# Gate products of the RG-LRU's tiles 0 to 5 on the two halves of the array's rows, their results brought to place by DMA

## The chip, the core and the metric

The kernel runs on one core of a Trainium2 chip. The metric is the device time of one execution in microseconds. A NeuronCore has a matrix engine (TensorE; PE in the profile, PEld for its weight loads), VectorE (DVE), ScalarE (ACT), GpSimd (POOL) and SyncE (SP), which issues the DMAs of this kernel. Each engine takes its instructions in the order of its own list. On-chip data lie in SBUF over 128 partitions; products land in PSUM, also 128 partitions.

## The reference, cut to what matters

One decoder layer over 1024 tokens and 1024 channels: a norm, an input projection, an S5 branch and an RG-LRU branch side by side, a gated merge, a SwiGLU feed-forward and a final gate. The change touches the RG-LRU branch alone. It works on 16 heads of 64 channels:

```python
xh = xc.reshape(bsz, L, LRU_HEADS, LRU_HEAD_DIM)          # 16 heads of 64
r = sigmoid(einsum('blhi,hij->blhj', xh, w_r) + b_r)
ig = sigmoid(einsum('blhi,hij->blhj', xh, w_i) + b_i)
log_a = -LRU_C * r * softplus(-lru_lambda)
a = exp(log_a)
bx = sqrt(-expm1(2.0 * log_a)) * ig * xh
h = scan(h -> a * h + bx)                                  # over the tokens
```

## The kernel before, in words

Channels lie on partitions, tokens on the free axis, so a tile is 128 channels by 1024 tokens, and the RG-LRU's 1024 channels are 8 tiles m of two heads each. A matrix product in full precision is made of three fp32r products (`mm3`, line 220): high part by high part, high by low and low by high, each in two pieces of 512 tokens. Weights come as 128x512 pieces: SP loads one (line 169), ACT makes its high part (195), DVE its low part (196).

A unit is one output tile: its products on PE, and behind them its evacuation `ev`, which is written into the program one unit later. For the gates of tile m, `ri_mm` (599) makes 12 products of 128x512 into two PSUM tiles of 1024 columns: one for r, one for i. Each weight block is 128x128 with the two heads' 64x64 matrices on its diagonal and zeros elsewhere. `ev_ri` (608) applies the two sigmoids (612) out of PSUM. After every odd m, `lru` (618) runs for the tiles m-1 and m: exponentials on ACT (623), tanh (626), squares (629), products on DVE (632, 634), square roots on ACT (636), a product (639) and the scan (643) on DVE, then a store of the scanned tile to DRAM for m below 6, which is read back later (722).

The order of the units around the change: input tile `ub` m (its 48 products, then u at 536 and 587, the convolution xc at 589 and 592 on DVE, and the split xch, xcl at 239 and 240), gates of tile m-2 (`RI_LAG` = 2), and after m = 2, 3, 5 and 6 one merge-gate tile. At the end come the gates of tile 6, a merge gate, the gates of tile 7, and the rest. The w_b_out products (from line 779) need all eight scanned tiles.

PSUM has four tiles of 1024 columns, shared by all units; a unit of the gates takes two. SBUF has 43 slots for tiles of 1024 columns, and five buffers each for the high and low weight parts. A framework puts the instructions of each engine, and the DMAs of SP, into one fixed list when the program is built, from times that it expects; at run time each engine takes its list in order and waits on semaphores. SP's list holds the weight loads too, and a load waits until the buffer that it fills has been read.

Of the kernel before, what the change touches and what calls it, by code (L numbers as in the profile page):

```python
# [14 lines left out]
AF = mybir.ActivationFunctionType  # L15
ALU = mybir.AluOpType

P = 128
L = 1024
# [14 lines left out]
GATES_FIRST = 10  # L34
UB_GATES = (2, 3, 5, 6)
RI_LAG = 2
S5_LAG = 4
S5_STAGGER = 3
X_POOL = ()
# [11 lines left out]
_n = 0  # L51
for _name, _cols in (
    ("g_mix", 8), ("b_in", 28), ("b_glu", 4), ("conv_w", 32), ("conv_b", 8),
    ("b_r", 8), ("b_i", 8), ("lam", 8), ("g_ffn", 8), ("g_pg", 8), ("b_pg", 8),
    ("g_ple", 8), ("g_fin", 8),
):
    VEC[_name] = _n
    _n += _cols
# [44 lines left out]
class Build:  # L103
# [343 lines left out]
    def plan(self):  # L447
        nc, h = self.nc, self.h
# [133 lines left out]
        xcs, xct, ri, yb = {}, {}, {}, {}  # L582
# [14 lines left out]
            return ev  # L597

        def ri_mm(m):
            def mm(u, hi, lo, pairs):  # L600
                u.ps = [self.ps_sm(), self.ps_sm()]
                for q in range(2):
                    w = slice((2 * (m % 2) + q) * P, (2 * (m % 2) + q + 1) * P)
                    self.mm3(u.ps[q], hi[:, w], lo[:, w], xcs[m], True, True)
                xcs.pop(m)
            return mm

        def ev_ri(m):
            def ev(ps):
                for q, b in ((0, "b_r"), (1, "b_i")):  # L610
                    t = self.slot(name="ri")
                    nc.scalar.activation(out=t, in_=ps[q], func=AF.Sigmoid, bias=self.v(b, m))  # L612
                    ri[m, q] = t
                if m % 2 == 1:
                    self.lru_last = self.start(lru(m - 1))
            return ev
# [33 lines left out]
        ri_elem = {}  # L650

        def add_ub(m):
# [3 lines left out]
                    self.lrup = self.start(self.lru_params())  # L656
            self.add(w_in(4 + m), ev_ub(m), pre=pre)

        def add_ri(m):
            if m // 2 not in ri_elem:  # L660
                ri_elem[m // 2] = self.elem(h["w_ri"][m // 2])
            self.add([(ri_elem[m // 2], None)], ev_ri(m), mm=ri_mm(m))


        ya, gl, mg, ybs = {}, {}, {}, {}
# [80 lines left out]
        for m in range(8):  # L746
            if m:
                add_ub(m)
            if m >= RI_LAG:
                add_ri(m - RI_LAG)  # L750
            if m in UB_GATES:
# [684 lines left out]
    def s5_data(self, hf):  # L1436
# [80 lines left out]
        yield  # L1517


INS = ("xT", "pT", "vec", "ident", "iota", "s5p", "s5bc", "s5d", "w_ple", "w_in", "w_ri", "w_glu", "w_a_out",  # L1520
       "w_b_out", "w_o", "w_gate", "w_up", "w_down", "w_pg")


# [6 lines left out]
def layout(a):  # L1530

    f = {}
    f["xT"] = np.ascontiguousarray(a["x"][0].T).reshape(8, P, L)
    f["pT"] = np.ascontiguousarray(a["p"][0, 0].T).reshape(2, P, L)
    cols = {
        "g_mix": a["g_mix"], "b_in": a["b_in"], "b_glu": a["b_glu"], "conv_w": a["conv_w"], "conv_b": a["conv_b"],
        "b_r": a["b_r"], "b_i": a["b_i"], "lam": a["lru_lambda"], "g_ffn": a["g_ffn"], "g_pg": a["g_ple_gate"],
        "b_pg": a["b_ple_gate"], "g_ple": a["g_ple"], "g_fin": a["g_final"],
    }
    f["vec"] = np.ascontiguousarray(np.concatenate([cols[n].reshape(-1, P) for n in VEC], 0).T)  # L1540
    f["ident"] = np.eye(P, dtype=np.float32)
    f["iota"] = np.tile(np.arange(P, dtype=np.float32), (P, 1))
    pair = lambda v: v.reshape(16, 2, 64).transpose(1, 2, 0).reshape(P, 16)
    ldt = np.repeat(a["log_dt"][0][:, None], 64, axis=1)
    f["s5p"] = np.ascontiguousarray(np.concatenate([pair(a["lam_re"][0]), pair(a["lam_im"][0]), pair(ldt)], 1))
    pb = lambda v: v.reshape(16, 2, 64, 16).transpose(1, 2, 0, 3).reshape(P, 16, 16)
    f["s5bc"] = np.ascontiguousarray(np.stack(
        [pb(a["s5_b_re"][0]), pb(a["s5_b_im"][0]),
         pb(a["s5_c_re"][0].transpose(0, 2, 1)), pb(a["s5_c_im"][0].transpose(0, 2, 1))], 1))
    d = np.zeros((2, 16, 16, 16), np.float32)  # L1550
    for i in range(16):
        d[:, i, :, i] = a["s5_d"][0].reshape(16, 2, 16)[:, :, i].T
    f["s5d"] = d.reshape(32, 16, 16)
    f["w_in"] = strips(a["w_in"][0])
    wp = strips(a["w_ple"][0])
    f["w_ple"] = np.ascontiguousarray(wp.reshape(4, 2, P, 256).transpose(0, 2, 1, 3)).reshape(4, P, 512)
    ri = np.zeros((8, 2, 2, 64, 2, 64), np.float32)
    for q, n in enumerate(("w_r", "w_i")):
        w = a[n][0].reshape(8, 2, 64, 64)
        for i in range(2):  # L1560
            ri[:, q, i, :, i, :] = w[:, i]

    f["w_ri"] = np.ascontiguousarray(ri.reshape(4, 2, 2, P, P).transpose(0, 3, 1, 2, 4)).reshape(4, P, 512)
    for n, s in (("w_glu", "w_glu"), ("w_a_out", "w_a_out"), ("w_b_out", "w_b_out"), ("w_o", "w_o"),
                 ("w_gate", "w_ffn_gate"), ("w_up", "w_ffn_up"), ("w_down", "w_ffn_down"), ("w_pg", "w_ple_gate")):
        f[n] = strips(a[s][0])
    return f
# [16 lines left out]
```

## Time and profile before

| what | value |
|---|---|
| runs shown | 1465.94 us median of 3 (1462.96 to 1466.12) |
| the profiled execution's own time | 1471.47 us |
| its span, first to last instruction | 1469.7 us |
| mean granted TensorE clock | 0.978 |
| PE busy | 97% of the span |
| DVE busy, ACT busy | 58%, 38% |

Starts in the profile are microseconds from the first instruction. The units of the gates lie between 343 and 491 us. A row of a timeline gives the start, the busy time, the engine, the line, what is written from what, and in brackets the idle time before it with what ended it. The tile names: sm is a PSUM tile of the gates' products, mm that of other units, ri a gate tile, xch and xcl the parts of xc, whi and wlo those of a weight piece.

### The profile page before, as it was taken

To read this page: it belongs to the slowest core of one execution; us is meant where nothing else is said; L and a number is where in the kernel's file an instruction comes from. 1 tells how busy PE (TensorE), PEld (TensorE's weight loads), DVE (VectorE), ACT (ScalarE), POOL (GpSimd) and SP (SyncE) were. 2 spreads that over 40 slices of the span, in tenths; PEclk is the share of its full clock that TensorE was granted. 3 is DMA by queue.
4 is the path that set the end of the run, shared out by engine and by line. 5 is a ranking of instruction groups with operands and counts; after the bars stand their busy time and mean duration, and the time that the engine had idled before them with its cause. 6 is when DMAs were issued, how large, how long until landed. Compare 5 with 4: busy or idle time off the path is not lost.

```text
span 1469.7 us, 16824 instructions
## 1 busy us (share of the span) xinstructions
PE 1420.5 (97%) x6586; PEld 1175.7 (80%) x6586; DVE 848.3 (58%) x988; ACT 565.8 (38%) x722; POOL 165.6 (11%) x250
## 2 busy tenths in 40 slices
PE   8999989999988899998999999999999999999995
PEld 6788877888877688887888888888888888888884
DVE  7367872635666864366556555556666243266586
ACT  7233235413665832244433333333335341133342
POOL 7910700000000000000000000000000021012333
PEclk9999979999999999999999999999999999999997
DMA  8224324451212554352122222222217342233222
GB/s 336 93 101 117 106 67 139 139 211 59 86 58 87 192 180 150 122 172 101 43 84 75 86 86 86 87 86 86 86 65 278 128 157 65 74 104 111 65 79 115
DMA packets 72047, 167.70 MB, mean 114 GB/s; under 512 B 11712, under 2 KB 23392, under 8 KB 71968
## 3 DMA queue, kind: packets, MB, share of 16 engines
q1 hardware_dynamic: 71968, 166.62, 33.6%
q8 instruction: 52, 0.85, 0.2%
q14 instruction: 27, 0.22, 0.0%
HBM read 121.37 MB, written 44.04 MB: 113 GB/s over the span
## 4 chain that ended last, share of the span: by engine, by line
PE 79%; issue 5%; ACT 5%; DVE 5%; POOL 4%; SPq 1%; DMA 1%; DVEq 0%; POOLq 0%; ACTq 0%
PE mm L228 46%; PE mm L321 29%; PE sm L1505 1%; PE sm L1500 1%; PE sm L228 1%; POOL x L1004 1%; SPq L1404 1%; ACT ri L612 1%; POOL el L1066 0%; DVE yb L643 0%; DVE x L1067 0%; DVE xc L592 0%; SPq L1444 0%; DVE el L1057 0%; ACT a L623 0%
## 5 line engine op out<-in xcount | busy, mean ns | idle before, releaser
L195 ACT ACTIVATE whi<-raw 128x512 fp32r<-128x512 f32 (+1 forms) x158 | 97.2, 617 | 360.7 <-PE mm L228 302.4
L321 PE MATMUL mm<-twh,whi 128*128 128x512 f32 x528 | 206.7, 392 | 3.8 <-ACT twh L239 3.8
L321 PE MATMUL mm<-twl,whi 128*128 128x512 f32 x528 | 206.4, 391 | 0.0
L321 PE MATMUL mm<-twh,wlo 128*128 128x512 f32 x528 | 202.9, 391 | 0.0
L196 DVE TENSOR_TENSOR wlo<-raw,whi 128x512 fp32r<-128x512 f32 (+1 forms) x158 | 111.6, 708 | 136.2 <-ACT whi L195 135.6
L228 PE MATMUL mm<-xgh,whi 128*128 128x512 f32 x448 | 141.7, 398 | 4.4 <-ACT ri L612 4.4
L228 PE MATMUL mm<-xgh,wlo 128*128 128x512 f32 x448 | 139.3, 393 | 0.9 <-DVE wlo L196 0.9
L228 PE MATMUL mm<-xgl,whi 128*128 128x512 f32 x448 | 140.0, 393 | 0.0
L321 PEld LDWEIGHTS mm<-twh,whi 128*128 128x128 f32 x528 | 99.7, 189 | 25.2 <-ACT twh L239 4.3
L321 PEld LDWEIGHTS mm<-twl,whi 128*128 128x128 f32 x528 | 99.9, 189 | 20.9
L321 PEld LDWEIGHTS mm<-twh,wlo 128*128 128x128 f32 x528 | 99.7, 189 | 20.8
L424 POOL TENSOR_TENSOR acc<-acc,sq 128x1024 f32<-128x1024 f32 (+1 forms) x18 | 43.3, 2406 | 610.4 <-DMA raw<-w_down 465.3
L228 PE MATMUL mm<-vh,wlo 128*128 128x512 f32 x352 | 108.9, 390 | 0.0
L182 ACT ACTIVATE whi<-wr 128x512 fp32r<-128x512 f32 x110 | 69.4, 631 | 102.6 <-PE mm L321 98.8
L228 PE MATMUL mm<-vl,whi 128*128 128x512 f32 x352 | 108.4, 389 | 0.0
L228 PE MATMUL mm<-vh,whi 128*128 128x512 f32 x352 | 108.3, 389 | 0.0
L228 PEld LDWEIGHTS mm<-xgh,whi 128*128 128x128 f32 x448 | 85.1, 191 | 23.4 <-ACT ri L612 4.9
L228 PEld LDWEIGHTS mm<-xgl,whi 128*128 128x128 f32 x448 | 85.6, 191 | 18.3 <-issue 0.2
L228 PEld LDWEIGHTS mm<-xgh,wlo 128*128 128x128 f32 x448 | 84.8, 190 | 19.2 <-DVE wlo L196 1.3
L183 DVE TENSOR_TENSOR wlo<-wr,whi 128x512 fp32r<-128x512 f32 x110 | 74.5, 685 | 25.0 <-ACT whi L182 24.9
L228 PEld LDWEIGHTS mm<-vh,wlo 128*128 128x128 f32 x352 | 66.1, 188 | 14.0 <-issue 0.2
L228 PEld LDWEIGHTS mm<-vh,whi 128*128 128x128 f32 x352 | 66.1, 188 | 13.9 <-issue 0.2
(389 smaller groups left out, 2456.8 us busy)
## 6 DMA issues: line engine op xcount, KB each, us to landing
raw<-w_in SPq DMA_DIRECT2D x56, 256.0 KB, 2.7
wr<-w_gate SPq DMA_DIRECT2D x22, 512.0 KB, 5.1
wr<-w_up SPq DMA_DIRECT2D x22, 512.0 KB, 3.6
vd<-fv SPq DMA_DIRECT2D x22, 512.0 KB, 2.9
vr<-vd SPq DMA_DIRECT2D x22, 512.0 KB, 5.5
raw<-w_down SPq DMA_DIRECT2D x32, 256.0 KB, 2.7
el<-ed SPq DMA_DIRECT2D x16, 512.0 KB, 4.2
x<-xT SPq DMA_DIRECT2D x8, 512.0 KB, 7.1
```

Of the source, the lines that this page charges most:

```text
L182: nc.scalar.activation(out=hi, in_=src, func=AF.Copy)
L183: nc.vector.tensor_tensor(out=lo, in0=src, in1=hi.bitcast(F32), op=ALU.subtract)
L195: nc.scalar.activation(out=hi[:, :w], in_=raw[:, :w], func=AF.Copy)
L196: nc.vector.tensor_tensor(out=lo[:, :w], in0=raw[:, :w], in1=hi[:, :w].bitcast(F32), op=ALU.subtract)
L228: nc.tensor.matmul(ps[:, t - t0:e - t0], w, v[:, t:e], start=(first and q == 0), stop=(last and q == 2),)
L321: nc.tensor.matmul(bank[b], w[:, k * P:(k + 1) * P], v, start=start and k == 0 and p == 0, stop=k == 3 and p == 2, skip_group_check=True)
L424: eng.tensor_tensor(out=a, in0=a, in1=s, op=ALU.add)
L612: nc.scalar.activation(out=t, in_=ps[q], func=AF.Sigmoid, bias=self.v(b, m))
L1004: (nc.gpsimd if eng else nc.vector).tensor_tensor(out=x, in0=x, in1=rstd["z"][:, :TAIL_CUT], op=ALU.mult)
L1404: nc.sync.dma_start(km[i][16 * j:16 * j + 16, :, (7 - j) * 16:P], ks[16 * i:16 * i + 16, :, 0:(j + 1) * 16])
L1500: nc.tensor.matmul(ps[:, o:o + P], km[hh][:, pr, :], us[q][:, 2 * i + hh, :], start=True, stop=False)
L1505: nc.tensor.matmul(ps[:, o + 1:o + P], G(w[hs, pr]), x[hs, pr * P:pr * P + 127], start=False, stop=last)
```

## The change

For the tiles m = 0 to 5 (`RI_HALVES` = 6) the products no longer use the block-diagonal weights. The weight block of tile m, from a new input `w_rh`, holds head 0's matrices on rows 0 to 63 with r and i side by side in the columns, and head 1's on rows 64 to 127 with i first. Each product then takes 64 rows: rows 0 to 63 write one PSUM tile, rows 64 to 127 the other, in turns, so there are again 12 products of 512 columns, each with half the rows. A PSUM tile now holds one head's r and i on its two halves of partitions, with the bias from a new table `b_ri`. The sigmoids write into two new tiles rx, and four DMAs of 64 partitions by 4 KB (256 KB each) build the r tile and the i tile from them. Six tiles make 24 such DMAs. The tiles 6 and 7 stay as they were.

The new weights come in two pieces (tiles 0 to 3, and 4 and 5) in place of three; all of the gates' weight pieces now lie in slots (`keep`) from their load to their last use, and no longer in the weight buffers. The table of vectors grows by 16 columns.

```diff
+RI_HALVES = 6
...
+            def halves(u, hi, lo, pairs):
+
+                u.ps = [self.ps_sm(), self.ps_sm()]
+                c = slice((m % 4) * P, (m % 4 + 1) * P)
+                xh, xl = xcs.pop(m)
+                for p, (w, v) in enumerate(((hi, xh), (hi, xl), (lo, xh))):
+                    for t in range(0, L, 512):
+                        for i in range(2):
+                            k = slice(64 * i, 64 * i + 64)
+                            self.nc.tensor.matmul(u.ps[i][:, t:t + 512], w[k, c], v[k, t:t + 512],
+                                                  start=p == 0, stop=p == 2)
+            return halves if m < RI_HALVES else whole
...
+                if m < RI_HALVES:
+                    t = [self.slot(name="rx") for _ in range(2)]
+                    for i in range(2):
+                        nc.scalar.activation(out=t[i], in_=ps[i], func=AF.Sigmoid, bias=self.v("b_ri", 2 * m + i))
+                    for q in range(2):
+                        o = ri[m, q] = self.slot(name="ri")
+                        for i in range(2):
+                            j = 64 * (i ^ q)
+                            nc.sync.dma_start(o[64 * i:64 * i + 64], t[i][j:j + 64])
...
         def add_ri(m):
-            if m // 2 not in ri_elem:
-                ri_elem[m // 2] = self.elem(h["w_ri"][m // 2])
-            self.add([(ri_elem[m // 2], None)], ev_ri(m), mm=ri_mm(m))
+            e, w = (m // 4, h["w_rh"][m // 4]) if m < RI_HALVES else (2 + m // 2, h["w_ri"][m // 2])
+            if e not in ri_elem:
+                ri_elem[e] = self.elem(w)
+                self.keep.add(ri_elem[e])
+            e = ri_elem[e]
+            self.add([(e, None)], ev_ri(m), mm=ri_mm(m))
+            if m in (3, RI_HALVES - 1, 7):
+                done(self.units[-1], e)
```

## Rows read from the trace of the kernel before

**Rows 1.** The page: span, busy time of PE, and the chain by engine.
```profile
span 1469.7 us, 16824 instructions
PE 1420.5 (97%) x6586; PEld 1175.7 (80%) x6586; DVE 848.3 (58%) x988; ACT 565.8 (38%) x722; POOL 165.6 (11%) x250
...
PE 79%; issue 5%; ACT 5%; DVE 5%; POOL 4%; SPq 1%; DMA 1%; DVEq 0%; POOLq 0%; ACTq 0%
```

**Rows 2.** Windows: stretch, its length, then busy time and instructions of each engine.
```profile
380.00:420.00 40.00, 36.08 (x153) 29.44 (x152) 28.95 (x26) 22.87 (x24) 0.00 (x0) 0.96 0.23 79
...
460.00:500.00 40.00, 35.56 (x146) 28.89 (x145) 26.37 (x24) 33.10 (x34) 0.00 (x0) 0.91 0.38 129
```

**Rows 3.** Waits of PE, 330 to 600 us: total, times, longest.
```profile
PE mm L228 <- ACT ri L612: 4.4, 1, 4.4
PE sm L228 <- ACT ri L612: 3.9, 1, 3.9
```

**Rows 4.** Windows, tile sm alone: the gates of tile 0.
```profile
343.87:346.59 2.72, 2.71 (x12) 2.06 (x11) 0.00 (x0) 0.00 (x0) 1.00 0.01 3
```

**Rows 5.** Windows: full-row products of L1500, then half-row ones of L1505.
```profile
226.60:227.38 0.78, 0.78 (x8) 0.75 (x7) 0.00 (x0) 0.00 (x0) 0.00 (x0) 1.00 0.40 92
227.38:228.66 1.28, 1.28 (x18) 1.07 (x16) 0.00 (x0) 0.00 (x0) 0.00 (x0) 1.00 1.02 350
```

**Rows 6.** Timeline of PE, 390 to 480 us.
```profile
392.84 0.61 PE L228 MATMUL sm<-xch,whi 128*128 128x512 f32 x2
...
411.88 1.22 PE L228 MATMUL sm<-xch,whi 128*128 128x512 f32 x2 [3.92 <-ACT ri L612]
...
414.61 0.88 PE L228 MATMUL mm<-xgh,whi 128*128 128x512 f32 x2
...
471.17 1.22 PE L228 MATMUL mm<-xgh,whi 128*128 128x512 f32 x2 [4.44 <-ACT ri L612]
```

**Rows 7.** The chain that ended last, in order of time: start, length, what.
```profile
368.52 2.72 PE sm L228 x12
...
377.90 2.00 ACT ri L612 x2
...
391.69 1.07 ACT ri L636
...
400.73 1.13 DVE u L536
...
408.35 0.05 ACT xch L239
...
410.71 1.12 ACT ri L612
...
472.14 1.28 ACT L623
...
513.21 3.02 PE mm L228 x8
```

**Rows 8.** Timelines of DVE (first four) and ACT (last), 381 to 404 us.
```profile
387.94 1.23 DVE L632 SCALAR_TENSOR_TENSOR ri<-a,ri 128x1024 f32<-128x1024 f32 x1 [0.69 <-ACT a L629]
392.78 1.23 DVE L639 TENSOR_TENSOR ri<-ri,ri 128x1024 f32<-128x1024 f32 x1 [3.61 <-ACT ri L636]
...
400.64 1.20 DVE L536 TENSOR_TENSOR u<-mm,rb 128x1024 f32<-128x1024 f32 x1
403.06 0.82 DVE L589 TENSOR_SCALAR xc<-u,vec 128x1024 f32<-128x1024 f32 x1 [1.22 <-ACT u L587]
...
381.21 2.20 ACT L623 ACTIVATE a<-ri,m8sp 128x1024 f32<-128x1024 f32 x2
```

**Rows 9.** DMA issues, KB and median us to landing; last, SP's timeline.
```profile
gbd<-gb SPq DMA_DIRECT2D x8, 512.0 KB, 2.9
raw<-w_ri SPq DMA_DIRECT2D x4, 256.0 KB, 2.6
km<-ks SPq DMA_DIRECT2D x4, 64.0 KB, 2.3
...
390.40 0.33 SPq L569 DMA_DIRECT2D gbd<-gb  x1
```

**Rows 10.** Waits of SP's queue, 455 to 490 us.
```profile
SPq L169 <- DVE wlo L196: 26.9, 4, 21.7
```

More of the change, by code (lines that the diff above doesn't have):

```diff
@@ L53 @@
     ("g_mix", 8), ("b_in", 28), ("b_glu", 4), ("conv_w", 32), ("conv_b", 8),
-    ("b_r", 8), ("b_i", 8), ("lam", 8), ("g_ffn", 8), ("g_pg", 8), ("b_pg", 8),
+    ("b_r", 8), ("b_i", 8), ("b_ri", 16), ("lam", 8), ("g_ffn", 8), ("g_pg", 8), ("b_pg", 8),
     ("g_ple", 8), ("g_fin", 8),
@@ L599, in ri_mm, with whole @@
         def ri_mm(m):
-            def mm(u, hi, lo, pairs):
+            def whole(u, hi, lo, pairs):
                 u.ps = [self.ps_sm(), self.ps_sm()]
@@ L605, in mm @@
                 xcs.pop(m)
-            return mm
+            def halves(u, hi, lo, pairs):
[9 more added lines that the diff above has]
+            return halves if m < RI_HALVES else whole
         def ev_ri(m):
             def ev(ps):
[L610 to L613, printed above, removed]
+                if m < RI_HALVES:
[7 more added lines that the diff above has]
+                            nc.sync.dma_start(o[64 * i:64 * i + 64], t[i][j:j + 64])
+                else:
+                    for q, b in ((0, "b_r"), (1, "b_i")):
+                        t = self.slot(name="ri")
+                        nc.scalar.activation(out=t, in_=ps[q], func=AF.Sigmoid, bias=self.v(b, m))
+                        ri[m, q] = t
                 if m % 2 == 1:
@@ L657, in add_ub, with done, f @@
             self.add(w_in(4 + m), ev_ub(m), pre=pre)
-        def add_ri(m):
-            if m // 2 not in ri_elem:
-                ri_elem[m // 2] = self.elem(h["w_ri"][m // 2])
-            self.add([(ri_elem[m // 2], None)], ev_ri(m), mm=ri_mm(m))
+        def done(u, e):
+            mm = u.mm
+            def f(u, *args):
+                mm(u, *args)
+                self.hi.pop(e), self.lo.pop(e)
+            u.mm = f
+        def add_ri(m):
+            e, w = (m // 4, h["w_rh"][m // 4]) if m < RI_HALVES else (2 + m // 2, h["w_ri"][m // 2])
[6 more added lines that the diff above has]
+                done(self.units[-1], e)
         ya, gl, mg, ybs = {}, {}, {}, {}
@@ L1517, in s5_data @@
         yield
-INS = ("xT", "pT", "vec", "ident", "iota", "s5p", "s5bc", "s5d", "w_ple", "w_in", "w_ri", "w_glu", "w_a_out",
+INS = ("xT", "pT", "vec", "ident", "iota", "s5p", "s5bc", "s5d", "w_ple", "w_in", "w_ri", "w_rh", "w_glu", "w_a_out",
        "w_b_out", "w_o", "w_gate", "w_up", "w_down", "w_pg")
@@ L1534, in layout @@
     f["pT"] = np.ascontiguousarray(a["p"][0, 0].T).reshape(2, P, L)
+    br, bi = (a[n][0].reshape(8, 2, 64) for n in ("b_r", "b_i"))
     cols = {
         "g_mix": a["g_mix"], "b_in": a["b_in"], "b_glu": a["b_glu"], "conv_w": a["conv_w"], "conv_b": a["conv_b"],
-        "b_r": a["b_r"], "b_i": a["b_i"], "lam": a["lru_lambda"], "g_ffn": a["g_ffn"], "g_pg": a["g_ple_gate"],
+        "b_r": a["b_r"], "b_i": a["b_i"], "b_ri": np.stack([br[:, 0], bi[:, 0], bi[:, 1], br[:, 1]], 1), "lam": a["lru_lambda"], "g_ffn": a["g_ffn"], "g_pg": a["g_ple_gate"],
         "b_pg": a["b_ple_gate"], "g_ple": a["g_ple"], "g_fin": a["g_final"],
@@ L1561, in layout @@
             ri[:, q, i, :, i, :] = w[:, i]
+    rh = np.stack([a["w_r"][0].reshape(8, 2, 64, 64), a["w_i"][0].reshape(8, 2, 64, 64)], 3)
+    rh[:, 1] = rh[:, 1, :, ::-1]
+    f["w_rh"] = np.ascontiguousarray(rh.reshape(2, 4, P, P).transpose(0, 2, 1, 3)).reshape(2, P, 512)
     f["w_ri"] = np.ascontiguousarray(ri.reshape(4, 2, 2, P, P).transpose(0, 3, 1, 2, 4)).reshape(4, P, 512)
```

## The prediction

> **What bounds the kernel now.** I read the page first: PE is busy for 97% of the span, and 79% of the chain that ended last is PE's own work [rows 1]. A product saved is therefore worth its time, except where PE waits for somebody else behind it. So the second view is busy time by stretch, over the units of the gates: in two stretches of 40 us PE does only 36.08 and 35.56 us of work [rows 2]. The third, PE's waits, names the cause: twice in this region PE waits for a sigmoid of L612, 3.9 and 4.4 us [rows 3]. The sigmoid is what frees a PSUM tile. The timeline puts the first wait in the middle of the gates of tile 3 (until 411.88) and the second behind the gates of tile 6 (until 471.17) [rows 6]. The reader should see that whatever is saved between the start of the chain that ends such a wait and the wait itself only makes the wait longer.
>
> The chain of waits shows where those chains start. The first begins at the end of input tile 3 (368.52), goes through the sigmoids of tile 1 (377.90), the lru of tiles 0 and 1 on ACT and DVE (square root at 391.69), u of tile 4 on DVE (400.73), its split (408.35) and the sigmoid of tile 2 at 410.71 [rows 7]. From 472.14 on the chain is nearly all ACT and DVE until w_b_out's products start at 513.21 [rows 7]; ACT is busy 33.10 of 40 us there [rows 2]. It starts at the end of input tile 7.
>
> **The change, part by part.** *The products.* A unit's 12 products take 2.72 us, 0.227 each [rows 4]. After, the same 12 instructions have 64 rows each. Does a pair on two row halves run side by side? The S5 products at L1505 are of that kind, alternating halves. Between full-row products of the same length, which begin every 0.111 us (seven begin in 0.78 us, and an eighth reaches in), 16 half-row ones end within 1.28 us, where one after the other would need 16 x 0.111 = 1.78 [rows 5]. As eight pairs they need 0.89, so going to half rows and back cost 0.39. For 512 columns I take six pairs of 0.227 and one 0.39: 1.75 us, which is 0.97 saved per unit, 5.8 in six. Bounds: pairs without the switch cost, 1.36 saved; no pairing at this length or type, 0.39 lost per unit.
>
> *Where a saving reaches the end.* The first chain starts behind the gates of tile 0, so that saving passes: -0.97. Those of tiles 1 and 2 fall into the wait until 411.88 and lengthen it. In tile 3 the first half now runs ahead of the wait [rows 6]; after, both PSUM tiles are needed at once, so all 12 products run behind it. Behind the idle the clock is low: the six products after the wait took 2.73 us (411.88 to 414.61 [rows 6]) against 1.36, and the stretch shows a mean granted clock of 0.96 [rows 2]. Six pairs at that pace take about the same 2.7 us, so tile 3 gives nothing. Tile 4 lies between the two waits: -0.97. Tile 5 lies behind the start of the second chain and only lengthens the second wait. On the path: -1.94.
>
> *The order on DVE.* DVE idles 3.61 us before it starts L639 at 392.78, and then does both scans before it evacuates u of tile 4 at 400.64 [rows 8]; yet input tile 4 was done on PE at 392.84 [rows 6], 0.06 us too late for the gap. After, two units are shorter, so PE is done at 392.84 - 1.94 = 390.90, while L639, which moves with the chain, is ready at 392.78 - 0.97 = 391.81 or, with the copies below, later. An order made from such times would put u into the gap. Then DVE's later work, 7.86 us from L639 to u [rows 8], ends at 399.67, and the convolution with what lies in between (403.06 to the split at 408.35, 5.29 us [rows 7, 8]) at 404.96: 3.39 us earlier in all, 2.42 beyond the 0.97. I take this: on the path now -0.97 - 2.42 - 0.97 = -4.36. Between 0 and 2.42 I choose the upper end since the gap is open in both times and only the fixed list could keep u behind the scans.
>
> *The copies.* Four DMAs per unit, 24 in all, on SP. No row shows this copy; the nearest are 64 KB between two SBUF tiles, 2.3 us to landing, and 256 KB from DRAM, 2.6; 512 KB took 2.9 [rows 9]. I take 2.6, bounds 2.3 and 2.9, and 0.33 for an issue [rows 9]. The r tile needs the first two, of which the second can only start with the second sigmoid's end: 0.33 + 2.6 = 2.9 us. The i tile has landed 0.66 later. Who waits: ACT has both exponentials of the pair queued. The sigmoids end at 379.90 [rows 7], the first exponential starts at 381.21 and the second at half of 2.20 later, 382.31 [rows 8]; r lands at 379.9 + 2.9 = 382.8, 0.5 late. Behind the second stand the tanh, the squares and the square roots, which are on the first chain; the tanh of the earlier tile could go first, so the cost is 0 to 0.5, and I take 0.5. The same in the pair of tiles 4 and 5 costs the last chain 0.5; the pair of 2 and 3 leads to no wait of PE. On DVE the product with xc (L634) waits for the i tile until 383.5. It had been ready earlier, and the next product of the pair ends at 387.94 + 1.23 = 389.17 with 3.61 us of idle behind it [rows 8]: nothing, as long as that gap stands. +1.0 in all.
>
> *Small parts.* One weight piece fewer to load and split, the longer vector table, and the slots of the kept weights and of rx: I price them at nothing, because ACT and DVE have idle time around them [rows 2]; the waits of PE in this stretch name no weight load [rows 3]. What is moved past in SP's queue: 24 issues of 0.33 us delay loads by at most 1.3 us at a time, and SP stands waiting for buffers for 26.9 us of 35 [rows 10].
>
> **Sum.** -4.36 + 1.0 = -3.4 us. The profiled execution took 1471.47 us (span 1469.7 and 1.8 around it), 5.5 above the median shown; it goes to 1468.1, and the median from 1465.94 to 1462.6. My bounds for this case, 1459 to 1464.5, come from 1.36 or 0.7 per unit and copies at 0 to 2 us.
>
> **Rivals.** *The order stays.* u remains behind the scans: -1.94 + 1.0 = -0.9, so 1465.0, no change. For it: lists are fixed from expected, not from measured, times. Against it: the gap of 3.61 us.
>
> *The first wait goes.* If the sigmoids of tile 2, whose products end at 392.84 + 2.72 = 395.56, no longer stand behind the split of tile 4 on ACT, the PSUM tile is free in time. Then the 3.92 us of idle and the 1.37 of low clock go, and five units count (4.85): -10.1 with no copy exposed, 1455.8. Against it: in the trace they stood behind that split, at 410.71 [rows 7].
>
> *The copies are held in SP's queue: slower.* SP waits 21.7 us at one stretch for a weight buffer in the stretch of the gates of tiles 5 and 6 [rows 10]. Copies of tile 5 that stand behind such a load keep ACT from the exponential, and that is on the last chain, where each microsecond of ACT's delay counts. The gain of 3.4 is gone from 3.4 us of such delay; the whole 21.7 would bound it from above. I price it at 6.5, a third of it: +3.1, so 1469.0. Against it: the list is made by expected times, and stores of other units, such as the one at 390.40 [rows 9], left as soon as their data were there.
>
> *The copies run one behind the other.* If the second copy starts only when the first has landed, r is there 2.6 us later than I took [rows 9], and both pairs pay it: +5.2 - 3.4 = +1.8, so 1467.7, no change. Against it: no row shows a copy that waits for the one before it. The Trainium skill (SBUF — State Buffer, "Door 1: The DMA port swizzle" and "Can I just issue two DMAs to hit both halves?") speaks for it: a transfer over 64 partitions reaches half the ports, and two to the two halves run one behind the other. An estimate from that page's 196 GB/s is 1.3 us per copy beside about 2 fixed, r after 4.7 us, and a sum near +0.2. No row of this trace shows a copy of 64 partitions.
>
> *No pairing.* If products of this type do not run side by side, a unit costs 0.39 more; with the copies +0.8 + 1.0, so 1467.7: no change. Rows 5 speak against it.
>
> **Chances.** Forecast 0.38, the order stays 0.24, the first wait goes 0.12, copies held 0.16, copies one behind the other 0.05, no pairing 0.05. A measurement of this kernel tells about 0.2%, 2.9 us. Faster: 0.36 of the forecast and the 0.12. Slower: 0.15 of the held copies and 0.02 each of the last two. The rest, 0.33, is no change. The range reaches from the first wait gone to copies held: 1456 to 1469.
>
> **What would show it.** Right: a unit of gates 0 to 5 takes about 1.75 us on PE, with pairs starting almost together; u of tile 4 stands ahead of the two scans on DVE; the wait in front of the gates of tile 3 is there, longer than 3.9 us, but ends near 408.5; w_b_out's products start near 510. Wrong: ACT waiting for a DMA into ri for more than a microsecond, SP holding copies behind a weight load, or the two waits unchanged in their place.

## The result, and the profile after

The changed kernel is **slower**: 1472.67 us median of 4 runs (1472.22 to 1473.07) against 1465.29 of the kernel before beside it, ratio 1.0053, 95% interval [1.0035, 1.0070]. The forecast of 1462.6 missed by 10 us, and the range of 1456 to 1469 does not hold the time. The profiled execution took 1473.07 us.

One thing has to be known before two traces are laid side by side. The S5 products between 190 and 234 us, long before the gates, take 34.0 to 34.6 us from the first to the last in 15 of the 18 traces and 38.7 in the other three (the first profile of the kernel before, e2 and e4), with the clock that TensorE was granted there. Below, the windows of the execution that the prediction was made from, and of a repeat of the same kernel (b_again, below); the seventh number is the granted clock:

```profile
190.00:234.00 44.00, 40.29 (x247) 33.59 (x247) 23.70 (x24) 10.89 (x12) 0.00 (x0) 0.77 0.34 102
```

```profile
190.00:234.00 44.00, 40.29 (x268) 33.62 (x267) 23.74 (x25) 14.35 (x15) 0.00 (x0) 0.88 0.38 111
```

As many us of work, but 21 products more done in them. So traces are compared from the first product of the gates on, and against the repeat. From there to the last product of the kernel it is 1115.5 us in the repeat (341.64 to 1457.16) and 1121.0 in the changed kernel (341.48 to 1462.43): 5.4 of the 6.2 us between the two profiled executions. They split so: until the gates of tile 5, 1.5 us **won** (115.8 us after, 117.4 before); from there to the end of PE's second wait, 6.0 us **lost** (16.0 against 10.0); behind it, 1.0 lost (989.1 us to the last product, 988.1 in the repeat; but the first profile of the kernel before takes 988.9 there, so this last part is hardly clear of the spread).

The page after, answering to [rows 1], and the windows of the units of tiles 0 and 1 and of the two stretches of [rows 2]:

```profile
span 1471.3 us, 16856 instructions
PE 1417.3 (96%) x6586; PEld 1167.7 (79%) x6586; DVE 847.5 (58%) x987; ACT 565.8 (38%) x721; POOL 165.0 (11%) x250
```

```profile
341.48:343.07 1.59, 1.59 (x14) 1.05 (x13) 1.49 (x2) 0.56 (x2) 0.00 (x0) 1.00 0.02 5
365.05:366.64 1.59, 1.59 (x14) 1.05 (x13) 1.48 (x2) 0.56 (x2) 0.00 (x0) 1.00 0.00 0
380.00:420.00 40.00, 35.90 (x147) 27.86 (x146) 28.86 (x26) 19.51 (x21) 0.00 (x0) 0.91 0.33 100
460.00:500.00 40.00, 30.16 (x116) 23.84 (x115) 24.31 (x21) 28.11 (x28) 0.00 (x0) 0.87 0.43 134
```

A unit takes 1.59 us in place of 2.72 [rows 4]: the halves run in pairs. The change to half rows and back also delays the products on either side of the unit: from the gates of tile 0 to those of tile 1 it is 23.57 us (341.48 to 365.05) in place of 24.48 (341.64 to 366.12 in the repeat), so a paired unit saves 0.91 us. But in the second stretch PE now does 30.16 us of work where it did 35.56, and the granted clock falls from 0.91 to 0.87. PE's waits from 330 to 600 us, and the places of the three longest on its timeline:

```profile
PE mm L229 <- ACT rx L626: 5.2, 1, 5.2
PE sm L229 <- DVE u L537: 4.6, 1, 4.6
PE sm L617 <- ACT rx L626: 4.1, 1, 4.1
```

```profile
401.31 0.73 PE L617 MATMUL sm<-xch,wkeep 64*128 64x512 f32 x2
...
407.07 1.22 PE L617 MATMUL sm<-xch,wkeep 64*128 64x512 f32 x2 [4.10 <-ACT rx L626]
...
465.19 1.22 PE L229 MATMUL sm<-xch,wkeep 128*128 128x512 f32 x2 [4.62 <-DVE u L537]
...
473.33 1.22 PE L229 MATMUL mm<-xgh,whi 128*128 128x512 f32 x2 [5.21 <-ACT rx L626]
```

The first wait is the old one, in the middle of the gates of tile 3. It ends 2.4 us earlier against the first gate product, 65.6 us after it in place of 68.0; by the gates of tile 4 only 0.6 of this is left (92.3 against 92.9 in the repeat). The seven microseconds behind the wait's end show where it goes: the repeat, then e2 of the experiments below, which has the copies and the old products, then the kernel after; the granted clock stands behind the five engines:

```profile
409.64:416.64 7.00, 7.00 (x24) 5.59 (x25) 5.94 (x7) 3.02 (x4) 0.00 (x0) 0.76 0.25 78
```

```profile
413.48:420.48 7.00, 7.00 (x24) 5.58 (x25) 1.50 (x2) 3.02 (x4) 0.00 (x0) 0.76 0.74 186
```

```profile
407.07:414.07 7.00, 7.00 (x16) 5.11 (x17) 1.50 (x2) 2.50 (x3) 0.00 (x0) 0.52 0.76 188
```

The mean granted clock there is 0.52 in place of 0.76: PE stays longer at 1.2 GHz, the lower of its two levels, and gets 16 products in place of 24. What came first behind the wait were six products of 64 rows, where it had been six of 128. From the wait's end to the gates of tile 4 it is 24.8 and 24.9 us in the two profiles of the kernel before and 24.9 in e2, but 26.05 to 27.41 in every trace with the half-row products, with copies or without.

The second wait has become two, and a name is new there: u, the evacuation of an input tile on DVE. DVE's timeline says why u is late. First the repeat of the kernel before, then the kernel after (L634 is now L657, L639 is L662, the scan L643 is L666, L536 is L537, L589 is L590):

```profile
454.54 1.23 DVE L634 TENSOR_TENSOR ri<-ri,xc 128x1024 f32<-128x1024 f32 x1 [1.07 <-ACT ri L612]
...
459.19 1.23 DVE L536 TENSOR_TENSOR u<-mm,rb 128x1024 f32<-128x1024 f32 x1 [1.88 <-PE mm L228]
...
461.64 0.81 DVE L589 TENSOR_SCALAR xc<-u,vec 128x1024 f32<-128x1024 f32 x1 [0.62 <-ACT u L587]
```

```profile
389.64 2.36 DVE L662 TENSOR_TENSOR ri<-ri,ri 128x1024 f32<-128x1024 f32 x2 [1.68 <-ACT ri L659]
391.92 4.47 DVE L666 TENSOR_TENSOR_SCAN yb<-a,ri 128x1024 f32<-128x1024 f32 x2
396.30 1.20 DVE L537 TENSOR_TENSOR u<-mm,rb 128x1024 f32<-128x1024 f32 x1
...
414.52 1.23 DVE L657 TENSOR_TENSOR ri<-ri,xc 128x1024 f32<-128x1024 f32 x1 [4.10 <-DMA ri<-rx]
...
462.18 1.23 DVE L657 TENSOR_TENSOR ri<-ri,xc 128x1024 f32<-128x1024 f32 x1 [4.01 <-DMA ri<-rx]
463.32 0.68 DVE L197 TENSOR_TENSOR wlo<-raw,whi 128x512 fp32r<-128x512 f32 x1
463.92 1.22 DVE L537 TENSOR_TENSOR u<-mm,rb 128x1024 f32<-128x1024 f32 x1
...
466.36 0.81 DVE L590 TENSOR_SCALAR xc<-u,vec 128x1024 f32<-128x1024 f32 x1 [0.62 <-ACT u L588]
```

Input tile 7 was done on PE when the gates of tile 5 began, at 457.32. In both kernels the product i times xc of tile 4 stands in DVE's list ahead of the evacuation of that input tile. Before, its data were there and it was done long before u was wanted. Now it waits for i's copies until 462.18, and u, the convolution, the split of xc on ACT, the sigmoids of tile 5 behind that split and so the PSUM tile that PE wants all follow late. DVE's waits and the copies' own rows:

```profile
DVE ri L657 <- DMA ri<-rx: 19.6, 6, 7.2
```

```profile
L631 SPq DMA_DIRECT2D ri<-rx x24: 467/588/1810, 351.0 to 475.1; - x24
...
DMA to landing us min/median/max: 3.1/4.3/5.6
```

An issue took 0.59 us in the median where I had put 0.33, and a copy 4.3 us to land where I had put 2.6 [rows 9]. The copies of a tile land one behind the other. Those of tile 4, issued at 455.35, 455.86, 456.55 and 457.19, land 3.1, 3.8, 4.3 and 4.9 us after the start of their issue, so at 458.5, 459.7, 460.9 and 462.1, each 1.2 us behind the one before. The first and the last of them:

```profile
DMA to landing us min/median/max: 3.1/3.1/3.1
...
DMA to landing us min/median/max: 4.9/4.9/4.9
```

### The profile page after: what moved, and what is told of

Same layout as the page of the kernel before. It is cut to its first block, busy times and chain, and to the rows that moved or that the text cites. A ratio compares the mean times of both kernels' runs of the same rounds, so it can differ in the third digit from the quotient of the medians.

```text
span 1471.3 us, 16856 instructions
## 1 busy us (share of the span) xinstructions
PE 1417.3 (96%) x6586; PEld 1167.7 (79%) x6586; DVE 847.5 (58%) x987; ACT 565.8 (38%) x721; POOL 165.0 (11%) x250
## 4 chain that ended last, share of the span: by engine, by line
PE 79%; DVE 6%; ACT 5%; issue 5%; POOL 4%; DMA 1%; SPq 0%; DVEq 0%; ACTq 0%; POOLq 0%
PE mm L229 46%; PE mm L322 29%; PE sm L1537 1%; PE sm L1542 1%; DVE xc L593 1%; POOL x L1041 1%; DVE yb L666 1%; PE sm L405 0%; POOL el L1103 0%; DVE x L1104 0%; PE sm L617 0%; DVE el L1094 0%; ACT sq L423 0%; ACT ri L659 0%; ACT L659 0%
## 5 line engine op out<-in xcount | busy, mean ns | idle before, releaser
L197 DVE TENSOR_TENSOR wlo<-raw,whi 128x512 fp32r<-128x512 f32 (+1 forms) x154 | 108.6, 708 | 136.6 <-ACT whi L196 136.6
L229 PEld LDWEIGHTS mm<-xgh,whi 128*128 128x128 f32 x448 | 84.6, 191 | 26.6 <-ACT rx L626 5.9
L184 DVE TENSOR_TENSOR wlo<-wr,whi 128x512 fp32r<-128x512 f32 x110 | 74.7, 687 | 24.9 <-ACT whi L183 24.9
```

The costliest lines, as they stand in the source:

```text
L184: nc.vector.tensor_tensor(out=lo, in0=src, in1=hi.bitcast(F32), op=ALU.subtract)
L197: nc.vector.tensor_tensor(out=lo[:, :w], in0=raw[:, :w], in1=hi[:, :w].bitcast(F32), op=ALU.subtract)
L229: nc.tensor.matmul(ps[:, t - t0:e - t0], w, v[:, t:e], start=(first and q == 0), stop=(last and q == 2),)
```

## The experiments

The kernel before ran beside each: its median was 1464.85 beside b_again to e3, 1465.56 beside e4 to e7, 1465.11 beside e8 to e11 and 1465.03 beside e12 to e19. The theories at the start: **A**, DVE stands behind the copies ahead of the next input tile's u; **B**, the products, the kept weights and the new tables cost; **C**, traffic and SP's list cost. **D**, the list of weight pieces, came from the trace of e1. The table has the copies' median time to landing, the time from the gates of tile 5 to the end of PE's second wait, and the time from the first gate product to the last product of the kernel; the last two are of the one profiled execution, the median is of all runs.

| run | what runs | median us | ratio, 95% interval | landing | tile 5 to 2nd wait's end | first gate to last |
|---|---|---|---|---|---|---|
| b_again | before | 1465.66 | 1.0009 [0.9996, 1.0022] | - | 10.0 | 1115.5 |
| after | the change | 1472.67 | 1.0053 [1.0035, 1.0070] | 4.3 | 16.0 | 1121.0 |
| e1 | products alone | 1465.60 | 1.0008 [0.9997, 1.0020] | - | 11.7 | 1115.5 |
| e2 | copies alone | 1476.68 | 1.0087 [1.0069, 1.0104] | 4.3 | 17.2 | 1126.4 |
| e3 | after, DVE's order | 1468.67 | 1.0025 [1.0010, 1.0041] | 4.4 | 11.7 | 1114.5 |
| e4 | after, four tiles | 1468.30 | 1.0017 [1.0005, 1.0028] | 4.4 | 12.4 | 1116.1 |
| e5 | e1, list as before | 1465.01 | 0.9988 [0.9976, 0.9999] | - | 9.9 | 1113.7 |
| e6 | after, r written directly | 1476.07 | 1.0062 [1.0042, 1.0081] | 3.0 | 17.0 | 1124.4 |
| e7 | e3 + list + r directly | 1471.99 | 1.0043 [1.0028, 1.0058] | 3.0 | 15.4 | 1121.6 |
| e8 | after, copies by GpSimd | 1477.28 | 1.0083 [1.0070, 1.0096] | 5.0 | 17.7 | 1126.8 |
| e9 | e11, copies by GpSimd | 1473.40 | 1.0056 [1.0043, 1.0068] | 4.7 | 13.1 | 1124.3 |
| e10 | after, 2 whole copies | 1465.17 | 0.9998 [0.9988, 1.0008] | 3.3 | 11.6 | 1114.0 |
| e11 | e3 + list | 1469.21 | 1.0031 [1.0021, 1.0041] | 4.4 | 9.9 | 1117.4 |
| e12 | after, 4 full-width copies | 1469.34 | 1.0032 [1.0021, 1.0043] | 2.5 | 14.0 | 1117.0 |
| e15 | e11, two queues | 1468.59 | 1.0026 [1.0017, 1.0035] | 3.8, 5.2 | 11.2 | 1117.6 |
| e18 | e11, 2 whole copies | 1464.94 | 1.0002 [0.9988, 1.0015] | 3.3 | 9.9 | 1115.2 |
| e19 | e11, four tiles | 1465.75 | 1.0003 [0.9992, 1.0014] | 4.4 | 10.0 | 1114.1 |

The one execution with a profile need not be a middle one: of e3's twelve runs (1464.95 to 1474.02) it was the second fastest. Where median and trace differ, the median is the verdict.

### The two halves of the change by themselves

**b_again** is the kernel before, unchanged.

> The kernel before, unchanged, for a second profile of it. The first one took 1471.5 us where its median is 1465.3, and its stretch 195 to 234 us shows a granted clock of 0.76. If that stretch is what varies between executions, the second profile shows a higher clock there and starts the gates of tile 0 some 4 to 6 us earlier (about 338 us), with the stretch 340 to 520 as before; then the changed kernel's loss against it lies in the gates. If the second profile is like the first up to 340 us, the changed kernel lost its time elsewhere.

It stands at 1.0009, no difference, and its trace is the one used above.

**e1, the products without the copies.** The two sigmoids' outputs are used as r and i; the values are not the reference's.

```diff
-                    t = [self.slot(name="rx") for _ in range(2)]
                     for i in range(2):
-                        nc.scalar.activation(out=t[i], in_=ps[i], ...)
-                    for q in range(2):
...
-                            nc.sync.dma_start(o[64 * i:64 * i + 64], t[i][j:j + 64])
+                        t = ri[m, i] = self.slot(name="ri")
+                        nc.scalar.activation(out=t, in_=ps[i], ...)
```

> The products on the row halves and the new weights and tables stay; the four copies of each tile go, and the two sigmoid tiles are used as r and i as they are (so r and i of the tiles 0 to 5 are not the reference's). Theory A (the copies hold up DVE, whose product of i with xc stands ahead of the next input tile's u): the loss goes, and the saving of the units between the two waits of PE stays: 1461 to 1464 us, second wait of PE ending about 10 us after the products of input tile 7. Theory B (the products or the kept weights cost, or the new tables at the start): 1470 to 1473. Theory C (only traffic and SP's list matter): as A.

**e2, the copies without the products:** the kernel before, with the sigmoids of tiles 0 to 5 writing into rx and the four copies of the change behind them, so that r and i are mixed up.

> The kernel before with the copies alone: the old products on all rows, two sigmoid tiles rx, and the same four half-tile copies in the same pattern for the tiles 0 to 5 (so the gates of these tiles are mixed up and not the reference's). Theory A: slower than the kernel before by at least as much as the changed kernel, 1472 to 1476, with DVE waiting 4 us or more for a copy ahead of u of tile 7. Theory B: 1465, no change.

The products alone brought no change, where theory A had a gain; the copies alone cost 11.8 us of median (1476.68 against 1464.85). So the loss is the copies', and theory B is out as its cause. That the products win nothing even without copies was a miss, and is taken up with e5.

### Where the copies hurt

**e3, DVE's order.** The product i times xc of a tile is put behind the split of the newest input tile, so that it can't hold u.

```diff
+                self.xmark = self.last
...
-                nc.vector.tensor_tensor(out=ri[m, 1], in0=ri[m, 1], in1=xct.pop(m), op=ALU.mult)
+                with self.tc.issue_after(self.xmark):
+                    nc.vector.tensor_tensor(out=ri[m, 1], in0=ri[m, 1], in1=xct.pop(m), op=ALU.mult)
```

> The changed kernel with one order fixed by hand: on DVE the product of i with xc is put behind the split of the latest input tile, so that u and the convolution of that tile no longer stand behind a wait for the copies. Copies and products are unchanged. Theory A: the second wait of PE ends about 10 us after the products of input tile 7 and not 16, so about 6 us are back: 1465 to 1468. Theory C (copies slow the weight loads or hold SP's list): 1471 to 1474, no change. What remains over the products alone is then what the copies cost on ACT in the last chain, about 3 us.

The second wait ends 11.7 us behind tile 5's gates in place of 16.0, and half of the loss is back. Theory A has its place shown, and C, which had the loss unchanged, falls as the main cause. But half remains.

**e4, four tiles** (`RI_HALVES = 4`; tiles 4 and 5 as before).

> The changed kernel with halves for the gate tiles 0 to 3 alone; tiles 4 and 5 are computed as before, without copies. Theory A (the loss comes from the products i*xc of tiles 4 and 5, which stand on VectorE ahead of input tile 7 and wait for their copies): the time from tile 5's products to the end of PE's second wait falls from 16.0 us to 10 to 11, and the kernel comes out at 1464 to 1467. Theory C (each copy costs the same wherever it stands, by its traffic and its place in SP's list): four of six tiles keep two thirds of the loss, 1469 to 1471.

1468.30, between the two expectations: the ratio of 1.0017 is a third of the change's, not two thirds, so the copies of tiles 4 and 5 carry most; yet the wait ended after 12.4 us, not 10 to 11. Something besides the copies delays u of input tile 7.

### What eats the products' gain

In e1 ACT does not reach u of input tile 7 in time either, though DVE does. On ACT's timeline of e1 a weight split stands ahead of it and waits for its load, a piece of w_b_out:

```profile
458.75 0.63 ACT L196 ACTIVATE whi<-raw 128x512 fp32r<-128x512 f32 x1 [3.63 <-DMA raw<-w_b_out]
459.29 1.14 ACT L588 ACTIVATE u<-u,vec 128x1024 f32<-128x1024 f32 x1
```

The changed kernel shows the same (4.38 us of idle until 463.30); the repeat of the kernel before has no wait for a load there.

**e5, e1 with the weight list of before:** three pieces of two tiles each, not kept, in place of two.

```diff
-            e, w = (m // 4, h["w_rh"][m // 4]) if m < RI_HALVES else ...
...
-                self.keep.add(ri_elem[e])
...
+                w = h["w_rh"][m // 4][:, 256 * (m // 2 % 2):256 * (m // 2 % 2) + 256] if m < RI_HALVES else h["w_ri"][m // 2]
+                ri_elem[m // 2] = self.elem(w)
```

> The products alone, as in the run without copies (outputs of the sigmoids used as r and i, so the values are not the reference's), but with their weights in the kernel before's list: three pieces of two tiles each, loaded and split at the same places as before and not kept, instead of two kept pieces of four and two tiles. Theory D (the shifted list of weight pieces made ScalarE wait for a piece of the output weights ahead of input tile 7 and so ate what the products had gained): tile 5 to the end of PE's second wait falls from 11.7 to about 10 us, and the kernel comes out at 1461 to 1463.5. Theory B (what the products save does not reach the end at all): 1464 to 1467, as without this edit.

```profile
456.08 0.63 ACT L196 ACTIVATE whi<-raw 128x512 fp32r<-128x512 f32 x1 [1.29 <-issue]
457.74 1.15 ACT L588 ACTIVATE u<-u,vec 128x1024 f32<-128x1024 f32 x1 [1.03 <-DVE u L537]
```

The wait for the load is gone, the second wait ends after 9.9 us, and the ratio is 0.9988 [0.9976, 0.9999], an interval that ends just short of none; the medians differ by 0.6 us, and 1465.01 is above the 1461 to 1463.5 expected. In the traces e5 needs 1.8 us less than the repeat from the first gate to the last product: 0.2 until the gates of tile 4, 0.9 from there to those of tile 5, 0.1 until the second wait ends and 0.6 behind it, where two profiles of the kernel before differ by 0.7. Theory D is shown for the wait. What the products bring without any copies is one to two microseconds, at the edge of what these runs can tell.

### Fewer copies, another queue

**e6, r written directly.** r's halves lie on the right partitions already; four sigmoids on 64 partitions write r and i's source, and only i is copied, twice per tile.

```diff
+                    x, r, o = self.slot(name="rx"), self.slot(name="ri"), self.slot(name="ri")
+                    for t, n in ((x, 1), (r, 0)):
+                        for i in range(2):
+                            j = 64 * (i ^ n)
+                            nc.scalar.activation(out=t[j:j + 64], in_=ps[i][j:j + 64], ...)
+                    for i in range(2):
+                        nc.sync.dma_start(o[64 * i:64 * i + 64], x[64 - 64 * i:128 - 64 * i])
```

> The changed kernel with r written by the sigmoids themselves (its halves are on the right partitions already): four sigmoids on half the partitions in place of two whole ones, and two copies per tile, for i alone, in place of four. Theory A: the exponentials no longer wait for copies, but VectorE still waits for i, somewhat less, because two issues are gone: 12 to 15 us from tile 5 to the end of the second wait, 1468 to 1471. Theory C (traffic): half of the copies' loss, 1468 to 1469; if half-partition sigmoids cost ScalarE as much as whole ones and this reaches the end, some 2 us more.

**e7** has this, the order of e3 and the list of e5.

> All three edits together: the weights in the list of before, r written by the sigmoids (two copies a tile), and VectorE's product i*xc put behind the newest input tile's work. Theories A and D together: tile 5 to the end of the second wait about 10 us, and 1460 to 1463.5, a little under the kernel before. If either of them is wrong, or if the copies cost something by traffic: 1465 to 1469.

Both missed: 1476.07 and 1471.99. ACT's timeline of e6 gives the reason:

```profile
460.14 2.25 ACT L628 ACTIVATE rx<-sm,vec 64x1024 f32<-64x1024 f32 x2
462.30 2.23 ACT L628 ACTIVATE ri<-sm,vec 64x1024 f32<-64x1024 f32 x2
```

Two sigmoids on 64 partitions take 2.25 us and two on 128 took 2.12, so a half costs as much as a whole; each tile costs ACT some 2.3 us more, and ACT is in both chains that end PE's waits. In e7 the gates of tile 5 begin 119.7 us after the first gate, against 116.2 in e5. Two copies instead of four landed in 3.0 us, which was not enough.

**e8, the copies on GpSimd's queue, e9 the same with order and list mended**, that is with DVE's order of e3 and the weight list of e5 (`nc.gpsimd.dma_start` in place of `nc.sync.dma_start`).

> The changed kernel with its copies issued on GpSimd's queue, which is idle in this stage, in place of SyncE's; nothing else differs. If the copies are late because their four issues stand one behind the other on SyncE among the weight loads and stores (theory C's second half): they land in about 3 us, the weight piece ahead of input tile 7 is no longer late, 1467 to 1470. If the transfer itself takes the time (theory A's price of about 4.3 us, whichever queue): VectorE waits as long as before, 1471 to 1474, and more if GpSimd's issue is slower than SyncE's.

> The weights in the list of before, VectorE's product i*xc behind the newest input tile's work, and the copies on GpSimd's queue; r and i both by copy, with whole sigmoids. Theories A and D: tile 5 to the end of the second wait about 10 us, 1462 to 1465.5, level with the kernel before or a little under. If the copies also hold the recurrence of tiles 4 and 5 at the end of the stage: 1466 to 1468.

Worse than with SP's queue: 5.0 and 4.7 us to landing, and here too the copies land one behind the other (those of tile 4 in e8 at 458.9, 460.8, 463.5 and 464.3). So SP's list alone was not what made them late.

**e11, order and list mended, the four copies on SP's queue.**

> The order of VectorE and the list of weight pieces together, with the changed kernel's four copies on SyncE's queue. Theories A and D: tile 5 to the end of the second wait about 10 us in place of 11.7, and 2 us less than with the order alone: 1465.5 to 1467.5. If D's late weight piece comes from the copies' place in SyncE's queue and not from the list: as with the order alone, 1468 to 1469.5.

The second wait is as short as before (9.9 us), and yet the median is 1469.21, no better than e3's; theory D's 2 us do not come out. PE's waits say what is late next: first the repeat of the kernel before, then e11:

```profile
PE mm L228 <- ACT ybh L239: 2.2, 1, 2.2
PE mm L228 <- ACT whi L195: 1.7, 1, 1.7
PE mm L228 <- DVE ybl L240: 0.3, 1, 0.3
```

```profile
PE mm L229 <- DVE ybl L241: 3.9, 2, 2.1
PE mm L229 <- ACT ybh L240: 2.4, 1, 2.4
```

All of them count: 4.2 us in the repeat (4.6 in the first profile), 6.3 in e11. The scans of tiles 4 and 5 start 1.9 us later against the first gate (147.5 us after it against 145.7), and PE, which reaches the products of yb earlier than before, waits there. It is not the order alone that delays them: in e18 below, with the same order and copies over all partitions, the first of these scans starts at 143.9. These waits are 2.1 of the 3.5 us that e11 needs more than the repeat behind the second wait; the rest was not taken apart.

### Why a copy takes 4.3 us

**e10, whole copies.** Two copies of 128 partitions per tile in place of four of 64, the same bytes; the halves are not exchanged, so the values are not the reference's.

```diff
-                        for i in range(2):
-                            j = 64 * (i ^ q)
-                            nc.sync.dma_start(o[64 * i:64 * i + 64], t[i][j:j + 64])
+                        nc.sync.dma_start(o, t[q])
```

> The changed kernel with two copies of whole tiles per gate tile in place of four of half tiles: the same bytes, all 128 partitions on both sides, two issues fewer; the halves are not exchanged, so the values are not the reference's. If a copy between 64 partitions is slow because it reaches half of the ports: whole copies of twice the bytes land in 4.3 us or less, i is there about 2 us earlier, 1466 to 1470. If bytes and issues set the time: landing 5 to 6 us for a copy, i about as late as before, 1470 to 1473.

```profile
455.75 1.23 DVE L655 TENSOR_TENSOR ri<-ri,xc 128x1024 f32<-128x1024 f32 x1 [1.68 <-DMA ri<-rx]
```

```profile
L629 SPq DMA_DIRECT2D ri<-rx x12: 465/471/532, 349.5 to 467.9; - x12
...
DMA to landing us min/median/max: 2.9/3.3/5.2
```

The whole loss is gone: 1465.17. Twice the bytes per copy landed in 3.3 us. The first issue for tile 4 was at 451.25, so i was there 4.5 us behind it; in the changed kernel it is 6.8 (455.35 to 462.18). And u of input tile 7 starts as early as in the kernel before.

**e12, four copies of 128 partitions and half the columns:** as many copies and bytes as the change.

> The changed kernel with four copies per gate tile of the same bytes as its own, each over all 128 partitions and half the columns (the halves are not exchanged, so the values are not the reference's). If the copies are slow because each touches 64 partitions on either side: they land in 3.5 us or less, as with two whole-tile copies, 1464.5 to 1467. If the number of issues and transfers sets it: landing 4 us or more, 1469 to 1472.

The rows of the copies and, on SP's timeline, the four issues of tile 4; below them the four issues of the changed kernel:

```profile
L631 SPq DMA_DIRECT2D ri<-rx x24: 470/593/613, 351.1 to 473.0; - x24
...
DMA to landing us min/median/max: 2.3/2.5/4.8
...
455.44 2.42 SPq L631 DMA_DIRECT2D ri<-rx  x4
```

```profile
455.35 3.00 SPq L631 DMA_DIRECT2D ri<-rx  x4
458.45 1.71 SPq L170 DMA_DIRECT2D raw<-w_b_out  x2
```

Here both theories were half right. The landing fell to 2.5 us, below the 3.5 that the width theory asked for: copies of the same size land 1.8 us sooner for spanning all partitions, and the last issue takes 0.61 us at most where it took 1.16 to 1.21 in five of six tiles. Neither the length of a row nor the crossing from one half to the other explains it: e10 has rows of 4 KB, as the change has, and of the change's four copies the two for r stay in their half and land as far apart as the two for i. The time did not follow all the way: the ratio fell from 1.0053 to 1.0032. The rest, from 1.0032 to e10's 0.9998, goes with two copies more per tile (four issues take 2.42 us one behind the other, two 1.47), but by which way is not shown: in both runs i of tile 4 is there 4.5 us behind the first issue. The product of tile 2 waits 3.33 us on DVE in e12 and 2.28 in e10, the sigmoids of tile 4 start 2.5 us later against the first gate, and u of input tile 7 is 2.6 us later.

**e15, both halves at once from two queues:** with order and list mended, the copies into the upper partitions are issued by ACT.

```diff
-                            nc.sync.dma_start(o[64 * i:64 * i + 64], t[i][j:j + 64])
+                            (nc.sync, nc.scalar)[i].dma_start(o[64 * i:64 * i + 64], t[i][j:j + 64])
```

> Order of VectorE and list of weights mended, and of each tile's four half copies the two into the lower partitions issued by SyncE, the two into the upper ones by ScalarE's queue. If a half copy is slow by the partitions that it reaches, and two at once on different queues reach all: landing about 3 us, 1464 to 1467, 2 to 4 us under the run with both edits and one queue (1469.2). If two queues share what one has, or ScalarE's issues delay its own chain: 1468 to 1472.

1468.59, as e11 within the intervals. The copies landed in 3.8 us on SP's queue and 5.2 on ACT's, and an issue held ACT for 1.00 us in the median and 2.37 at most. The copies still land in turn (those of tile 4 at 455.3, 456.4, 457.9 and 459.7): two queues gave no more than one.

The Trainium skill (SBUF — State Buffer, "Can I just issue two DMAs to hit both halves?") says that transfers to the two halves of the partitions run one behind the other, from whichever engine they are issued, and that only one transfer over all 128 partitions reaches every port. Here e8 and e15 agree with the first, with landings in turn from one queue or two, and e12 with the second, with landings 0.7 us apart in place of 1.2. An estimate from the same page's 196 GB/s for 64 partitions ("Door 1: The DMA port swizzle") and its roughly 2 us fixed ("The DMA setup-cost knee") is four copies of 1.3 us and 2, 7.2 us; the trace shows 6.8.

**e18, whole copies with order and list mended**, what the change would be if its copies could be made at full width, and **e19, order and list mended, halves for tiles 0 to 3 alone**, which keeps the reference's values.

> Order of VectorE and list of weights mended, with two whole-tile copies in place of four half ones (the halves are not exchanged, so the values are not the reference's): what the change would be with copies of the same bytes at full width. Theory: the products' gain of 1.8 us less at most 1 for the recurrence's end, 1462.5 to 1465. If the exponentials' wait for r at the end of the stage costs more: 1466 to 1468.

> Order of VectorE and list of weights mended, halves for the gate tiles 0 to 3 alone, so no copies near the second wait. Theories A and D: tile 5 to the end of the second wait about 10 us, 1463 to 1465.5, level with the kernel before or a little under. If copies in the first stretch cost something too: 1466 to 1468.

1464.94 and 1465.75: level with the kernel before, neither faster. Both have the long stretch behind the first wait (26.7 and 26.6 us to the gates of tile 4). At the products of yb PE waits 5.3 us in e18 and 3.9 in e19, 5.1 in e5 and 4.2 in the repeat: what else takes the products' gain in e18 is not shown. A single copy that exchanges the halves over all 128 partitions was not tried.

## Why the prediction was wrong

On the trace the time moved so against the repeat: 1.5 us won until the gates of tile 5, where the terms up to there add up to -4.36 + 0.5, then 6.0 lost until the second wait ends, where only 0.5 was priced, and 1.0 behind it.

**The products: right.** Forecast 0.97 us saved per unit, measured 0.91 (24.48 to 23.57 from gate to gate). The unit itself takes 1.59 and not 1.75, and the products on either side of it lose 0.22.

**Where a saving reaches the end: wrong at tile 3.** Two units were to pass, -1.94. In e5, which has the products alone, 0.2 of tile 0's is left at the gates of tile 4, and tile 4 adds 0.9; that e5's whole trace comes to 1.8 us is luck. "Tile 3 gives nothing" was the mis-sized term. The six half-row products behind the wait took 2.85 us (407.07 to 409.92), about as forecast; the list runs the other six before the wait (401.31), all unpaired. But the clock stays low longer behind them, and the stretch to the gates of tile 4 grows by 1.8 us (26.7 against 24.9; 26.4 in e5).

**The order on DVE: wrong.** This was the largest term, -2.42. The rows of after show both scans from 391.92 and u of tile 4 behind them at 396.30, so the rival that the order stays had u right. The list was not the same, though: the two weight splits that stood ahead of the scans (391.68 and 395.60 in the repeat) are gone from there, u starts 54.8 us after the first gate product where it started 56.8, and the first wait ends 2.4 us earlier, where -0.97 - 2.42 would have been 3.4.

**The copies' overlap: wrong, and the step that failed first.** I took 2.6 us to landing and 0.33 per issue, and let the four copies run side by side. The rows were those of single DMAs: 256 and 512 KB over 128 partitions, and 64 KB over 16. The first copy of a tile is near that (2.7 us from the end of its issue at 455.82), but each of the next lands 1.2 us later, so the median is 4.3 (3.1 to 5.6), and an issue takes 0.47 to 1.21, once 1.81. i is complete 5.9 us behind the second sigmoid's end (456.32 to 462.18), where the forecast had 3.6. The rival of copies running one behind the other had this mechanism; I gave it 0.05 because no row showed it, and priced it by the exponential alone.

**DVE's L634: wrong, and the step that cost the most.** "Nothing, as long as that gap stands" was worked out for the pair of tiles 0 and 1, and a gap is still there (1.68 us ahead of 389.64). But the same instruction stands five more times in DVE's list, and for tiles 2 and 4 what is queued behind it is the next input tile (4.10 and 4.01 us of wait). Of the 6.0 us that the second wait's end lost, e3 gives 4.3 back; the other 1.7 are the weight load's, below (11.7 in e3, 9.9 in e11). I asked what the wait of one copy costs, and not what stands behind each of the six.

**The exponential: right in kind.** 0.5 us was the price for each of two pairs; the waits were 2.27 us for tile 5 and 0.34 for another tile.

**Small parts: wrong.** One weight piece fewer was priced at nothing because waits of PE named no load. It moved a load of w_b_out to where ACT meets it ahead of u of input tile 7, 3.6 us of ACT's time in e1 (4.4 in after), and took what the products gain: 1.8 us at the second wait (11.7 in e1, 9.9 in e5).

**The rival on the slower side** (copies held in SP's queue behind a weight load) named the wrong holder: the copies left as their data came, and it was the weight load that stood behind them (issued at 458.45); it is late without any copies too, in e1. The 1.0 us behind the second wait were not taken apart. A third of the 21.7 us would have been 7.2, not 6.5, and with 1.36 per unit and copies at nothing the sum gives 1460.8, not 1459; neither changes the account.

## What to carry to other kernels

Before a result is moved by a copy, list every instruction that reads it and what stands behind each in its engine's list: a product that was harmless while its data were at hand holds the whole queue once they come late. Make copies span all partitions, and price one from a row of the same width; half a tile is not half the price. Price several copies in a row by the landing of the last, not of one. A saving that lies ahead of a wait is worth nothing there, so measure the saving alone (here one to two microseconds of the 5 x 0.91 that five paired units save on PE) before paying for it.

## What was not expected of the hardware

- Copies between SBUF tiles of 256 KB landed in 4.3 us over 64 partitions and in 2.5 over 128 (e12), four in a row each time; their landings were 1.2 and 0.7 us apart.
- An issue on SP took 0.33 us alone, 0.47 as the first of four copies, 0.59 as the second, and 1.16 to 1.21 as the fourth of the half-width copies in five tiles of six.
- The same copies issued by GpSimd landed in 5.0 us, and by ACT, behind two of SP's, in 5.2.
- Behind a wait of PE, six products of 64 rows ahead of full ones went with a granted clock of 0.52 over seven microseconds, six of 128 rows with 0.76.
- The granted clock of one stretch, 190 to 234 us, was 0.77 in one execution of the same kernel and 0.88 in another.
